# A row of 1 / rms for the gate: by way of HBM, in place of products with ones

## The chip, the cores and the metric

The kernel runs on one core of a Trainium2 chip. The metric is the device time of one execution in microseconds (us); each kernel is run several times and the median counts. The profile is of one execution by itself.

## The reference

One layer of a decoder on x of 1024 tokens by 1024 features, float32: an RMSNorm, gated linear attention (GLA) with 4 heads and chunks, a residual, another RMSNorm, a squared-ReLU MLP with 4096 hidden features, a residual, and a final RMSNorm. What the change touches is the gate of GLA:

```python
def rms_norm(x, g):
    y = x * lax.rsqrt(jnp.mean(x * x, axis=-1, keepdims=True) + EPS)
    return y * g
...
proj = h @ w_in                      # h = rms_norm(x, l0_norm_mix)
q, k, v, r, gk_low = jnp.split(proj, ...)
log_a = jax.nn.log_sigmoid(gk_low @ w_gk_up + b_gk) / GLA_GATE_NORM
```

gk_low has 16 columns (the gate's rank). 1 / rms is one number a token, and can be multiplied in after the product with w_in.

## The kernel before, in words

All big matrix products are done as seven products of half-sized blocks (Strassen's scheme), each of them in three passes of high and low parts so that float32 is kept. `step` does one such product: 4 lanes of 128 rows, each 4 times 3 matmuls of 128x512, so 48 matmuls. `chunks_of` runs a plan of such groups of seven steps; while step n runs on TensorE (PE), the operands of the next one are made by ScalarE (ACT, `split`: the high part) and VectorE (DVE: the low part; line 178: sums of blocks). `hooks` hang other work into a step: key (i, at) is the place before step `at` of group `i`, (i, at, "then") that after the next operands are made, and (i, at, lane, kp) a place between two matmuls of the step. The order on PE is the order in which the code is written; on the other engines a scheduler orders by the same program, and each queue, that of the DMA-issuing SyncE (SP) included, is worked off strictly in its order. DMAs share eight semaphores in turn, so a DMA also waits until the eighth one before it has landed.

Group 0 makes q and k, transposed (tokens in the free dimension), from the scaled but not normalized x; group 1 makes v. The split blocks of x are kept in HBM (`keep`, line 338, tiles xv: "keeps") and read back for group 1 (line 494). The loads of the weights for v are those of line 326.

What the gate needs, and the names that matter below:

- `gk_first` and `gk_second` multiply x's halves of 512 tokens with w_gk, transposed: the low-rank rows of the gate, with eight copies of 16 rows on 128 partitions, tokens along the free dimension.
- `token_rms` sums the squares of each token (ACT) and makes `rstd1` [128, 8], 1 / rms with the tokens on the partitions (`rstd_of`; its last instruction is line 114, DVE).
- The gate's rows have the tokens along the free dimension, so 1 / rms is needed as a row of 512 tokens on every partition. `spread_rms(hf)` makes it for one half: for each of 4 blocks of 128 tokens, DVE multiplies the identity with a column of `rstd1` (line 506), PE multiplies all ones with that (the product's rows are all the same: the diagonal), ACT copies the result from PSUM (line 508). Then DVE multiplies the gate's rows with it (line 513), ACT copies them to `gk` (line 514), and DVE leaves in partitions 64 to 127 the rest that the rounded copy lacks (line 515).
- `gate_in` multiplies `gk` with the split w_up (PE, "mm<-g,wup"), one matmul a head and half. The first one stands two lanes behind `spread_rms(0)`, within step 0 of group 1.

`spread_rms(0)` hangs at (1, 0, 0, 3), after the first lane of the first step for v; `spread_rms(1)` at (1, 5), after `gk_second`. In the order below and in the trace, "g" is a buffer of [128, 1024], "gl" and "mm" are PSUM banks, "big" holds a split operand, "wa" and "wb" weights, "vx" inputs and v.

Of the kernel before, what the change touches and what calls it, by code (L numbers as in the profile page):

```python
# [8 lines left out]
F32 = mybir.dt.float32  # L9
# [4 lines left out]
AF = mybir.ActivationFunctionType  # L14
ALU = mybir.AluOpType

P = 128
T = 1024
# [22 lines left out]
def order_after(tc, inst, other, wait=True):  # L41

    kind = mybir.DependencyClass.Sync if wait else mybir.DependencyClass.NoSync
    tc.add_manual_dep(inst.ins, other.ins.name, mybir.DependencyInfo(kind, mybir.DependencyReason.DATA),
                      reason="order of phases")
# [3 lines left out]
def hybrid_trunk(ctx: ExitStack, tc: tile.TileContext, x, xT, w_head, w_r, w_gk, w_up,  # L49
                 w_out, w_ff1, w_ff2, vecs, g_fin, out):  # L50
    nc = tc.nc
    act, dve, pe, pool = nc.scalar, nc.vector, nc.tensor, nc.gpsimd
    sb = ctx.enter_context(tc.tile_pool(name="sb", bufs=1))
    dram = ctx.enter_context(tc.tile_pool(name="dram", bufs=1, space=bass.MemoryType.DRAM))
# [5 lines left out]
    def new(tag, dtype=F32):  # L60
        count[0] += 1
        pool_ = ps if tag in ("mm", "gl") else sb
        return pool_.tile(SHAPE.get(tag, [P, 1024]), dtype, tag=tag, bufs=BUFS[tag], name=f"{tag}{count[0]}")

    def f32(ap):
        return ap.bitcast(F32)

    def mm(o, w, m, start, stop, partial=False):

        pe.matmul(o, w, m, start=start, stop=stop, skip_group_check=partial)  # L70
# [18 lines left out]
    ones = sb.tile([P, P], F32, name="ones")  # L89
# [6 lines left out]
    ident = sb.tile([P, P], F32, name="ident")  # L96
# [6 lines left out]
    def rstd_of(y, ss, n, cnt):  # L103

        m, t = new("st")[:, 0:n], new("st")[:, 0:n]
        act.activation(y, ss, AF.Ln, scale=1.0 / cnt, bias=eps)
        act.activation(y, y, AF.Exp, scale=-0.5)
        dve.tensor_scalar(m, ss, -0.5 / cnt, -0.5 * EPS, op0=ALU.mult, op1=ALU.add)
        if n == 1:
            dve.scalar_tensor_tensor(t, y, y, m, op0=ALU.mult, op1=ALU.mult)  # L110
        else:
            dve.tensor_tensor(t, y, y, op=ALU.mult)
            dve.tensor_tensor(t, t, m, op=ALU.mult)
        dve.scalar_tensor_tensor(y, t, 1.5, y, op0=ALU.add, op1=ALU.mult)
# [4 lines left out]
    def run(general):  # L119
        stat = {n: sb.tile([P, w], F32, tag=n, bufs=1, name=f"{n}{int(general)}")  # L120
                for n, w in dict(ss1=8, rstd1=8, ss2=8, rstd2=8, rstd3=8, tok=32, est=96).items()}
        ss1, rstd1, ss2, rstd2, rstd3 = (stat[n] for n in ("ss1", "rstd1", "ss2", "rstd2", "rstd3"))
# [5 lines left out]
        def half(hf):  # L128
            return slice(hf * 512, hf * 512 + 512)
# [291 lines left out]
        box = {}  # L421
# [9 lines left out]
        def token_rms(ts):  # L431
            for t in ts:
                xr = new("g4")
                nc.sync.dma_start(xr, x[t * P:(t + 1) * P, :])
                order_after(tc, act.activation(xr, xr, AF.Square, accum_out=ss1[:, t:t + 1]), last["split"], wait=False)
            if TT - 1 in ts:
                rstd_of(rstd1, ss1, 8, D)
                dve.tensor_tensor(r_sq, rstd1, rstd1, op=ALU.mult)
                dve.tensor_scalar(r_qs, r_sq, QS, None, op0=ALU.mult)
                dve.tensor_scalar(r_neg, rstd1, -1.0, None, op0=ALU.mult)  # L440
                dve.tensor_scalar(r_ss, r_sq, QS * QS / DV, None, op0=ALU.mult)

        qk, part = {}, {}

        def qk_view(a, h):

# [51 lines left out]

        def spread_rms(hf):

            u = new("g4")
            dg, rbc = u[:, 0:512], u[:, 512:1024]
            pb = new("mm")
            for c in range(4):
                cs = slice(c * P, c * P + P)
                dve.tensor_scalar(dg[:, cs], ident, rstd1[:, hf * 4 + c:hf * 4 + c + 1], None, op0=ALU.mult)
                mm(pb[:, cs], ones, dg[:, cs], True, True)
            act.activation(rbc, pb, AF.Copy)
            if hf == 0:
                box["gk"] = new("g4", F32R)  # L510
            raw, gk = box["raw"][hf], box["gk"][:, half(hf)]
            dst = raw if hf == 0 else dg
            dve.tensor_tensor(dst, raw, rbc, op=ALU.mult)
            act.activation(gk, dst, AF.Copy)
            dve.tensor_tensor(gk[64:128, :], dst[64:128, :], f32(gk[64:128, :]), op=ALU.subtract)
# [240 lines left out]
        def g(f, *args):  # L756
            return lambda: f(*args)
# [35 lines left out]
        def gk_second():  # L793
# [3 lines left out]
        wv = weight_side(True, from_v, dve, late=True)  # L797
        fine_steps.add((0, 0))
        hooks = {(0, 1): (gk_first,), (0, 3): (split_up,),
                 (0, 4): (g(token_rms, range(0, 4)),), (0, 5): (g(token_rms, range(4, 8)),),  # L800
                 (1, 0, 0, 3): (g(spread_rms, 0),),
                 (1, 2): (x12_load,), (1, 4): (x12_split,), (1, 5): (gk_second, g(spread_rms, 1))}
        if not general:
            hooks.update({(1, 0, 2, 3): (g(gate_in, 0, 0, "mm"), g(gate_in, 1, 0, "mm")),
                          (1, 0, 3, 3): (g(gate_in, 2, 0, "mm"),),
                          (1, 1, 0, 1): (g(gate_in, 3, 0, "mm"), g(prep_fast, 0, 0)),
                          (1, 2): (x12_load,),
                          (1, 2, "then"): (g(prep_fast, 1, 0),), (1, 3, "then"): (g(prep_fast, 2, 0),),
                          (1, 4): (), (1, 4, "then"): (g(prep_fast, 3, 0), x12_split),
                          (1, 5): (gk_second, g(spread_rms, 1)) + tuple(g(load_wr, 0, kq, "wa") for kq in range(4)),  # L810
                          (1, 6): tuple(g(f, a, kq, *tag) for f, a, kq, tag in
                                        [(split_wr, 0, kq, ()) for kq in range(4)]
                                        + [(load_wr, 1, kq, ("wa" if kq > 1 else "raw",)) for kq in range(4)]),
                          (1, 6, 2, 1): (g(gate_in, 0, 1, "mm"), g(prep_fast, 0, 1)),
                          (1, 6, 3, 1): (g(operands, 0, "mm"),)})
# [231 lines left out]
    with tc.manual_schedule(engines={mybir.EngineType.PE}):  # L1047
        run(False)
# [3 lines left out]
    with tc.If(go_general > 0):  # L1052

        level_mask = {}
        masks = new("at").bitcast(BF16)
        pool.memset(masks, 1.0)
        for n, s in enumerate(LEVELS):
            nb = 64 // s
            m = masks[:, n * 64:(n + 1) * 64].unsqueeze(1)
            mv = m.rearrange("p o (b t) -> p (o b) t", t=s)  # L1060
            pool.affine_select(mv, mv, [[-2 * s, nb], [0, s]], ALU.is_ge, 0.0, base=0, channel_multiplier=1)
            pool.affine_select(mv, mv, [[2 * s, nb], [0, s]], ALU.is_ge, 0.0, base=s - 1, channel_multiplier=-1)
            level_mask[s] = m
        run(True)
# [50 lines left out]
```

## Time and profile before

| | |
|---|---|
| median of 3 runs | 1020.11 us (1019.8 to 1021.35) |
| the profiled execution | 1020.24 us |
| its span, first to last instruction | 1018.4 us |
| PE busy | 1002.9 us, 98% |
| DVE, ACT, POOL busy | 721.9, 548.4, 191.2 us |
| mean granted TensorE clock | 0.995 |

A profile's line of a group or of the timeline gives the start (us from the start of the span), the length, the engine, the line of the kernel, the operation, and out<-in; in square brackets stands for how long the engine was idle before it, and who released it. PEld is the loading of weights, beside PE. SPq rows are DMAs being issued by SP: their length is the time of issuing, and the time until the data has landed is an answer of its own, on the DMAs. Float32 matmuls whose operands are not split are two records each.

### The profile page before, as it was taken

The page shows a single profiled execution, that of the slowest core. Times are in us where ns is not written, and L with a number is a line of the kernel's source. Part 1 is how long each engine was busy: PE and PEld are TensorE (multiplying, and loading weights), DVE is VectorE, ACT ScalarE, POOL GpSimd, SP SyncE. Part 2 cuts the span into 40 slices and gives each one's busy share as a digit, 9 for nine tenths or more (in the row PEclk, how much of TensorE's full clock was granted, in tenths as well). Part 3 has the DMA queues.
Part 4 walks back from the last instruction along what each step waited for, and adds up shares of the span by engine and source line. Part 5 has one row for each costly group of instructions (what it writes and reads, how often), then busy time and mean ns, then how long its engine had stood idle before and what let it go on. Part 6 is the DMA issues. An engine that isn't in the chain of part 4 may idle for free.

```text
span 1018.4 us, 12257 instructions
## 1 busy us (share of the span) xinstructions
PE 1002.9 (98%) x4618; PEld 835.9 (82%) x4618; DVE 721.9 (71%) x897; ACT 548.4 (54%) x828; POOL 191.2 (19%) x114
## 2 busy tenths in 40 slices
PE   8999999999999999999999999999999999999996
PEld 7788878888888888888888888888888888888884
DVE  4996686776568997979965338965339965339965
ACT  6785566666576457658332447332447332447355
POOL 0000010000000000041304341214341214341260
PEclk9999999999999999999999999999999999999998
DMA  8799796223236034573124762124762124861004
GB/s 266 277 332 378 268 305 192 83 84 104 83 92 200 20 104 181 210 283 133 42 83 165 283 236 101 42 83 165 285 244 91 41 83 165 294 240 45 1 1 169
DMA packets 103580, 164.28 MB, mean 161 GB/s; under 512 B 5336, under 2 KB 75096, under 8 KB 93272
## 3 DMA queue, kind: packets, MB, share of 16 engines
q1 hardware_dynamic: 102424, 162.75, 45.9%
q8 instruction: 38, 0.62, 0.2%
q10 hardware_dynamic: 1088, 0.67, 0.2%
q14 instruction: 30, 0.25, 0.1%
HBM read 127.74 MB, written 35.65 MB: 160 GB/s over the span
## 4 chain that ended last, share of the span: by engine, by line
PE 83%; DVE 1%; ACT 1%; issue 1%; ACTq 0%; DVEq 0%
PE gl L70 50%; PE mm L70 31%; PE mm L937 1%; PE gl L706 1%; PE gl L626 0%; DVE vx L902 0%; DVE big L82 0%; DVE g L927 0%; ACT g L1007 0%; ACT st L1008 0%; DVE st L1011 0%; ACT st L1009 0%; DVE g L1015 0%; PE mm L706 0%; ACT raw L1013 0%
## 5 line engine op out<-in xcount | busy, mean ns | idle before, releaser
L70 PE MATMUL gl<-big,big 128*128 128x512 f32 x2508 | 585.5, 390 | 3.3 <-ACT big L81 1.9
L70 PEld LDWEIGHTS gl<-big,big 128*128 128x128 f32 x2508 | 470.7, 188 | 101.6 <-DVE big L82 2.2
L70 PE MATMUL mm<-big,big 128*128 128x512 f32 x1188 | 279.7, 389 | 0.0
L70 PEld LDWEIGHTS mm<-big,big 128*128 128x128 f32 x1188 | 223.0, 188 | 46.3
L82 DVE TENSOR_TENSOR big<-wa,big 128x1024 fp32r<-128x1024 f32 (+1 forms) x118 | 159.4, 1377 | 107.1 <-ACT big L81 107.1
L81 ACT ACTIVATE big<-wa 128x1024 fp32r<-128x1024 f32 (+1 forms) x118 | 118.1, 1038 | 136.6 <-PE gl L70 66.6
L178 POOL TENSOR_TENSOR wa<-wa,wb 128x1024 f32<-128x1024 f32 x14 | 42.9, 3068 | 350.6 <-DVE big L82 350.6
L178 POOL TENSOR_TENSOR wa<-wa,wa 128x1024 f32<-128x1024 f32 x28 | 74.7, 2675 | 160.9 <-DVE big L82 159.6
L70 PE MATMUL mm<-big,wb 128*128 128x512 f32 x384 | 94.9, 397 | 0.0
L82 DVE TENSOR_TENSOR big<-hq,big 128x1024 fp32r<-128x1024 f32 x48 | 61.3, 1282 | 42.9 <-ACT big L81 42.8
L82 DVE TENSOR_TENSOR big<-wb,big 128x1024 fp32r<-128x1024 f32 x42 | 56.4, 1355 | 44.5 <-ACT big L81 44.3
L70 PEld LDWEIGHTS mm<-big,wb 128*128 128x128 f32 x384 | 70.6, 188 | 14.3
L81 ACT ACTIVATE big<-hq 128x1024 fp32r<-128x1024 f32 x48 | 48.5, 1052 | 54.0 <-PE gl L70 32.5
L81 ACT ACTIVATE big<-raw 128x1024 fp32r<-128x1024 f32 x44 | 45.7, 1058 | 55.3 <-DVE raw L178 28.3
L81 ACT ACTIVATE big<-wb 128x1024 fp32r<-128x1024 f32 x42 | 43.0, 1052 | 59.9 <-PE mm L70 33.2
L82 DVE TENSOR_TENSOR big<-raw,big 128x1024 fp32r<-128x1024 f32 x44 | 69.2, 1587 | 2.0 <-ACT big L81 2.0
L902 DVE TENSOR_TENSOR vx<-gl,vx 128x512 f32<-128x512 f32 x95 | 63.2, 681 | 6.1 <-PE gl L70 5.9
L178 POOL TENSOR_TENSOR wa<-wb,wa 128x1024 f32<-128x1024 f32 x14 | 41.1, 2947 | 44.7 <-DVE big L82 44.7
L546 POOL COPY top<-g 128x4 f32<-128x4 f32 x8 | 4.1, 518 | 204.4 <-DVE g L538 204.4
L960 ACT ACTIVATE hq<-hq 128x1024 f32<-128x1024 f32 x24 | 25.4, 1058 | 29.6 <-DVE hq L953 29.6
L70 PE MATMUL gl<-wb,wa 128*128 128x256 f32 x180 | 31.2, 304 | 0.0
L902 DVE TENSOR_TENSOR vx<-mm,vx 128x512 f32<-128x512 f32 x45 | 29.9, 680 | 1.5 <-PE mm L70 1.4
(183 smaller groups left out, 796.4 us busy)
## 6 DMA issues: line engine op xcount, KB each, us to landing
big<-xw SPq DMA_DIRECT2D x42, 1024.0 KB, 6.9
xv<-big SPq DMA_DIRECT2D x14, 1024.0 KB, 7.6
xw<-big SPq DMA_DIRECT2D x14, 1024.0 KB, 5.0
big<-xv SPq DMA_DIRECT2D x10, 1024.0 KB, 6.5
wb<-xv SPq DMA_DIRECT2D x32, 256.0 KB, 3.4
wb<-in_w_ff SPq DMA_DIRECT2D x32, 256.0 KB, 3.3
wa<-in_w_ff SPq DMA_DIRECT2D x32, 256.0 KB, 3.9
wa<-in_w_ff SPq DMA_DIRECT2D x16, 512.0 KB, 4.8
```

Source lines behind the costliest of these rows:

```text
L70: pe.matmul(o, w, m, start=start, stop=stop, skip_group_check=partial)
L81: last["split"] = act.activation(hi, src, AF.Copy)
L82: last["low"] = dve.tensor_tensor(lo, src, f32(hi), op=ALU.subtract)
L178: op = self.eng.tensor_tensor(*(self.ap(b, kp, 2) for b in (o, x_, y_)), op=op)
L546: pool.tensor_copy(top[:, 8 * h + 4 * hf:8 * h + 4 * hf + 4].unsqueeze(2), a[:, :, P - 1:P])
L706: pe.transpose(tp[:, h * P:(h + 1) * P], on[:, h * DV + j * P:h * DV + j * P + P], ident)
L902: return dve.tensor_tensor(xd, p_, xd, op=ALU.add)
L937: pe.transpose(p_[:, c * P:(c + 1) * P], xn[4 * hf + c][:, kt * P:(kt + 1) * P], ident)
L960: act.activation(d2, d2, AF.Relu)
```

## The change

The four products with ones and their diagonals are gone. `token_rms` stores `rstd1` to a row of 1024 numbers in HBM as soon as it is final (`rms_row`, a DMA on SP's queue, 128 partitions of 8 numbers, each number a piece of 4 bytes by itself, since neighbours on a partition are 128 tokens apart). `load_rms(hf)` reads 512 of them back onto all 128 partitions (256 KB into a g buffer, SP's queue). It hangs at (0, 6, "then") for the first half, and behind `x12_split` in (1, 4, "then") for the second. `spread_rms` multiplies with what was read. The hooks that run on this data are those under `if not general`.

```diff
@@ token_rms @@
                 rstd_of(rstd1, ss1, 8, D)
+                nc.sync.dma_start(rms_row.rearrange("o (t p) -> p (o t)", p=P), rstd1)
                 dve.tensor_tensor(r_sq, rstd1, rstd1, op=ALU.mult)
...
-        qk, part = {}, {}
+        rms_row = dram.tile([1, T], F32, name=f"rms{int(general)}")
+
+        def load_rms(hf):
+
+            if hf == 0:
+                box["rbc"] = {}
+            box["rbc"][hf] = new("g4")[:, 0:512]
+            nc.sync.dma_start(box["rbc"][hf], rms_row[:, half(hf)].to_broadcast([P, 512]))
+
+        qk = {}
...
         def spread_rms(hf):
 
-            u = new("g4")
-            dg, rbc = u[:, 0:512], u[:, 512:1024]
-            pb = new("mm")
-            for c in range(4):
-                cs = slice(c * P, c * P + P)
-                dve.tensor_scalar(dg[:, cs], ident, rstd1[:, hf * 4 + c:hf * 4 + c + 1], None, op0=ALU.mult)
-                mm(pb[:, cs], ones, dg[:, cs], True, True)
-            act.activation(rbc, pb, AF.Copy)
+            raw, rbc = box["raw"][hf], box["rbc"][hf]
             if hf == 0:
                 box["gk"] = new("g4", F32R)
-            raw, gk = box["raw"][hf], box["gk"][:, half(hf)]
-            dst = raw if hf == 0 else dg
+            gk = box["gk"][:, half(hf)]
+            dst = raw if hf == 0 else rbc
             dve.tensor_tensor(dst, raw, rbc, op=ALU.mult)
             act.activation(gk, dst, AF.Copy)
...
-                 (0, 4): (g(token_rms, range(0, 4)),), (0, 5): (g(token_rms, range(4, 8)),),
+                 (0, 4): (g(token_rms, range(0, 4)),), (0, 5): (g(token_rms, range(4, 8)),), (0, 6, "then"): (g(load_rms, 0),),
...
-                          (1, 4): (), (1, 4, "then"): (g(prep_fast, 3, 0), x12_split),
+                          (1, 4): (), (1, 4, "then"): (g(prep_fast, 3, 0), x12_split, g(load_rms, 1)),
```

The order on SP's queue, from the loads of v's weights (wa, wb, from in_w_head) to the end of the keeps (xv), in the kernel before:

```order
L326 DMA wb79_644<-in_w_head 128x2x256 x2
L326 DMA wb80_645<-in_w_head 128x2x256 x2
L338 DMA xv600_102<-big83_658 128x2048
L338 DMA xv610_103<-big84_661 128x2048
L326 DMA wa85_718<-in_w_head 128x2x256 x2
L326 DMA wa86_719<-in_w_head 128x2x256 x2
L326 DMA wb87_724<-in_w_head 128x2x256 x2
L326 DMA wb88_725<-in_w_head 128x2x256 x2
L338 DMA xv000_90<-big89_730 128x2048
L338 DMA xv010_91<-big90_731 128x2048
L338 DMA xv500_100<-big93_796 128x2048
L338 DMA xv510_101<-big94_797 128x2048
```

and the same place in the changed kernel, from the last of the first eight loads on (line 438 is the store of `rstd1`, line 451 the load of the row):

```order
L326 DMA wb80_647<-in_w_head 128x2x256
L438 DMA rms0_194<-rstd10_84 128x8x1
L326 DMA wb80_647<-in_w_head 128x2x256
L338 DMA xv600_102<-big83_660 128x2048
L338 DMA xv610_103<-big84_663 128x2048
L326 DMA wa85_720<-in_w_head 128x2x256 x2
L326 DMA wa86_721<-in_w_head 128x2x256 x2
L326 DMA wb87_726<-in_w_head 128x2x256 x2
L326 DMA wb88_727<-in_w_head 128x2x256 x2
L338 DMA xv000_90<-big89_732 128x2048
L338 DMA xv010_91<-big90_733 128x2048
L451 DMA g493_746<-rms0_194 128x512
```

The store has gone between the two halves of the eighth tile's loads (the seventh and the eighth load of 256 KB), and the load of the row between the second keep and the third of the last four. The store waits for `rstd1` to be final (line 114 on DVE), the load for the store's landing.

The order on ACT, where step 0 of group 1 is emptied from PSUM (line 476 before, 486 after: one bank a lane, into v's tile) and the gate's rows are copied to gk (line 514 before, 517 after); lines 527 and 528, or 530 and 531, read the first products with w_up. Before:

```order
L476 ACTIVATE vx100_827<-gl99_814,tok0_88 128x512
L508 ACTIVATE g4101_829<-mm102_830 128x512
L476 ACTIVATE vx105_857<-gl104_844,tok0_88 128x512
L514 ACTIVATE g4103_840<-g436_293 128x512
L476 ACTIVATE vx107_872<-gl106_859,tok0_88 128x512
L527 ACTIVATE g4109_876<-mm108_874,vec_63 128x512
```

and in the changed kernel:

```order
L486 ACTIVATE vx101_831<-gl100_818,tok0_88 128x512
L486 ACTIVATE vx104_850<-gl103_837,tok0_88 128x512
L486 ACTIVATE vx106_865<-gl105_852,tok0_88 128x512
L517 ACTIVATE g4102_833<-g436_294 128x512
L530 ACTIVATE g4108_869<-mm107_867,vec_63 128x512
L531 ACTIVATE g4108_869<-mm107_867,vec_63 128x512
```

The copy to gk has moved behind the emptying of the third lane. On DVE the sequence around it is as before, without the four products with the identity: the two sums of line 178, the multiplication of the gate's rows (line 513 before, 516 after), the subtraction (515, now 518).

More of the change, by code (lines that the diff above doesn't have):

```diff
@@ L799, in run @@
         hooks = {(0, 1): (gk_first,), (0, 3): (split_up,),
-                 (0, 4): (g(token_rms, range(0, 4)),), (0, 5): (g(token_rms, range(4, 8)),),
+                 (0, 4): (g(token_rms, range(0, 4)),), (0, 5): (g(token_rms, range(4, 8)),), (0, 6, "then"): (g(load_rms, 0),),
                  (1, 0, 0, 3): (g(spread_rms, 0),),
-                 (1, 2): (x12_load,), (1, 4): (x12_split,), (1, 5): (gk_second, g(spread_rms, 1))}
+                 (1, 2): (x12_load,), (1, 4): (x12_split, g(load_rms, 1)), (1, 5): (gk_second, g(spread_rms, 1))}
         if not general:
```

## Prediction

> **What bounds the kernel now.** The page comes first, then what PE waited for in the whole span.
>
> ```profile
> span 1018.4 us, 12257 instructions
> PE 1002.9 (98%) x4618; PEld 835.9 (82%) x4618; DVE 721.9 (71%) x897; ACT 548.4 (54%) x828; POOL 191.2 (19%) x114
> ```
> ```profile
> PE gl L70 <- ACT big L81: 1.9, 1, 1.9
> ...
> PE mm L70 <- DVE vx L474: 0.9, 1, 0.9
> ```
>
> TensorE is busy for 98% of the span, and its few waits are single ones of 1 to 2 us (columns: total, times, longest). So a microsecond taken from PE's queue is a microsecond won, and a new wait in that queue is lost in full: nothing later stands idle to give it back. The change touches PE's queue twice, so those two places are read in the timelines. PE first (start, length; one matmul with ones is two records, hence x8 for four):
>
> ```profile
> 93.45 1.05 PE L70 MATMUL mm<-g,ones 128*128 128x128 f32 x8
> 94.26 5.72 PE L70 MATMUL gl<-big,big 128*128 128x512 f32 x24
> 99.82 0.62 PE L70 MATMUL mm<-g,wup 128*128 128x512 f32 x2
> ...
> 152.10 1.05 PE L70 MATMUL mm<-g,ones 128*128 128x128 f32 x8
> 152.91 17.28 PE L70 MATMUL gl<-big,big 128*128 128x512 f32 x75
> ```
>
> PE goes straight through: the products with ones take from 93.45 to 94.26 and from 152.10 to 152.91, and 5.6 us after the first group come the gate's products with w_up (99.82), which read what spread_rms made. What DVE and ACT do for those:
>
> ```profile
> 79.30 0.16 DVE L114 SCALAR_TENSOR_TENSOR rstd<-st,rstd 128x8 f32<-128x8 f32 x1
> ...
> 94.79 2.36 DVE L178 TENSOR_TENSOR wa<-wa,wb 128x1024 f32<-128x1024 f32 x2
> 97.06 0.68 DVE L513 TENSOR_TENSOR g<-g,g 128x512 f32<-128x512 f32 x1
> 98.54 0.69 DVE L515 TENSOR_TENSOR g<-g,g 64x512 fp32r<-64x512 f32 x1 [0.80 <-ACT g L514]
> ```
> ```profile
> 97.30 0.69 ACT L476 ACTIVATE vx<-gl,tok 128x512 f32<-128x512 f32 x1 [2.16 <-PE gl L70]
> 97.89 0.62 ACT L514 ACTIVATE g<-g 128x512 fp32r<-128x512 f32 x1
> 100.02 0.69 ACT L476 ACTIVATE vx<-gl,tok 128x512 f32<-128x512 f32 x1 [1.51 <-PE gl L70]
> ```
>
> The gate's rows are ready when L515 ends, 98.54 + 0.69 = 99.23, and PE wants them at 99.82: 0.6 us of slack, no more. rstd1, the start of it all, is final at 79.46. That date matters for SP, whose queue the change uses:
>
> ```profile
> 76.06 0.87 SPq L338 DMA_DIRECT2D xv<-big  x2
> ...
> 87.61 2.58 SPq L338 DMA_DIRECT2D xv<-big  x4
> ```
>
> **Removed.** Two groups of products with ones: 94.26 - 93.45 = 0.81 us each, 1.62 us off PE. The eight DVE products with the identity and two ACT copies out of PSUM go too; I cost them at nothing, since DVE then waits for other work (the first group stands ahead of splits that wait for ACT's).
>
> **Added on SP: the store.** It is issued behind seven of the eight loads of wv (the order in the change, above), and waits there for L114, until 79.5. In the kernel before, SP came to this point between the seventh load (74.75 + 0.55, below) and the two keeps at 76.06. So SP stands for some 4 us, and behind it wait the eighth load, the keeps, eight more loads, four keeps and the row's own load. What does that do to the DMA rings? The seventh load and its landing (us from issue, last column of the second answer):
>
> ```profile
> 74.75 0.55 SPq L326 DMA_DIRECT2D wb<-in_w_head  x1
> ```
> ```profile
> wb<-in_w_head SPq DMA_DIRECT2D x1, 256.0 KB, 5.0
> ```
>
> It lands at 79.8, so the rings run dry just as the store goes out. After a keep a load of 256 KB lands 0.7 us later when the rings are full (keep issued 76.56, landed after 10.3; load issued 77.39, landed after 10.2), but 3.4 us after its issue when they are empty:
>
> ```profile
> 76.56 0.37 SPq L338 DMA_DIRECT2D xv<-big  x1
> 77.39 0.39 SPq L326 DMA_DIRECT2D wa<-in_w_head  x1
> 130.23 0.51 SPq L717 DMA_DIRECT2D wa<-in_w_r  x1
> ```
> ```profile
> xv<-big SPq DMA_DIRECT2D x1, 1024.0 KB, 10.3
> wa<-in_w_head SPq DMA_DIRECT2D x1, 256.0 KB, 10.2
> wa<-in_w_r SPq DMA_DIRECT2D x1, 256.0 KB, 3.4
> ```
>
> Before, the eighth load landed at about 79.8 + 0.7 = 80.5. After: store issued at 79.5, 0.8 us of issuing (the 512 pieces of the row at 130.23 took 0.51; the store has 1024), load issued at 80.3, landed 3.4 later at 83.7. The 1024 pieces of 4 bytes of the store stand ahead of it. No row here shows such a store. From below: nothing, because they move while the rings are idle anyway, and the smallest load, 128 rows of 88 bytes, lands like any other:
>
> ```profile
> vec<-in_vecs ACTq DMA_DIRECT2D x1, 11.0 KB, 3.5
> ```
>
> From above: a keep writes 128 rows of 8 KB to HBM in 2.4 us when the rings are full (below), 19 ns a row, and 1024 such rows would be 19 us. In between, 2 KB at a keep's rate are 4.8 ns, so 1024 are 4.9 us. The pieces are nearest to the smallest rows: w_r's 512 pieces pass within the 0.7 us of 256 KB, 1024 thus in 1.4 at most, and I take the middle of 0 and 1.4. Then the eighth load lands at 83.7 + 0.7 = 84.4, and everything behind it is 84.4 - 80.5 = **3.9 us late**. Who misses that? The eighth load feeds DVE's splits just ahead of L178 (94.79): nobody. The eight loads behind the keeps feed L178; they had landed by 92.8 (a keep queued behind them landed at 95.2, below, less its own 2.4), so now by 96.7, against 96.0 for L178's second half: 0.7 us on DVE, inside the wait that follows. The Trainium skill, page "DMA: Bandwidth & Descriptors", speaks against this store: by its Rules for kernel authors a strided last dim becomes one descriptor per element, and by its Specifications less than 512 B is a read-modify-write. No run here shows that yet; with the roughly 10.5 ns a packet of its section Bandwidth, 64 on each of 16 engines would be an estimate of 0.7 us.
>
> **Added on SP: the load of the row.** It stands behind the first two of the four keeps that began at 87.61. The first two of them landed so:
>
> ```profile
> 88.36 0.34 SPq L338 DMA_DIRECT2D xv<-big  x1
> ```
> ```profile
> xv<-big SPq DMA_DIRECT2D x1, 1024.0 KB, 7.6
> xv<-big SPq DMA_DIRECT2D x1, 1024.0 KB, 9.2
> ```
>
> that is at 87.61 + 7.6 = 95.2 and 88.36 + 9.2 = 97.6. The row's 256 KB follow 0.7 later, at 98.3 without the lateness: already past 97.06, when DVE wants them. With it the row lands at 98.3 + 3.9 = 102.2.
>
> **Moved on ACT.** In the new order ACT empties the third bank of the step before it copies the gate's rows. PE finishes that bank just before the w_up products, now at 99.82 - 0.81 = 99.0. The emptying starts 0.2 later (100.02 against 99.82), the copy 0.6 after that (97.89 - 97.30), DVE's subtraction 0.65 after that (98.54 - 97.89) and lasts 0.69: 101.1. So PE waits at least 101.1 - 99.0 = **2.1 us** even for a row that is on time.
>
> **The wait.** With the row at 102.2: multiplication (0.68), copy (0.65 to the subtraction), subtraction (0.69), and the handing over: 104.3. PE is there at 99.0, and waits 5.3 us. Behind the multiplication in DVE's queue stands the emptying of the next step's banks, which PE has yet to fill, so DVE's standing still costs nothing more.
>
> **The clock.** PE's gap is long enough for the clock (columns: length, PE busy, PEld, DVE, ACT, POOL, granted clock, DMA, GB/s):
>
> ```profile
> 4.75:8.16 3.41, 1.46 (x8) 0.85 (x8) 1.80 (x4) 1.35 (x2) 0.42 (x2) 1.00 0.99 311
> 8.16:11.57 3.41, 3.41 (x9) 2.64 (x10) 2.65 (x5) 2.52 (x5) 0.00 (x0) 0.50 0.88 259
> ```
>
> With 1.46 of 3.41 us busy, that is after a gap of 1.95 us, the next 3.41 us were granted half the clock: 9 matmuls where 15 would fit (24 take 5.56 us at 94.26). A gap of 5.3 us leaves such a stretch nearly empty, so I add half of 3.41, less what of it falls into the gap itself: between 0 and 1.7, taken as 1.2. The Trainium skill, "TensorE: Matmul & The Clock Gate", Part 1, gives the same consequence for an idle window of about 3.4 us; in this trace 1.95 us sufficed, and the measurement decides.
>
> **The second half** (152 us). Its row is loaded behind the last x12 store, which lands at 155.5:
>
> ```profile
> 149.90 0.53 SPq L791 DMA_DIRECT2D xv<-g  x1
> ```
> ```profile
> xv<-g SPq DMA_DIRECT2D x1, 512.0 KB, 5.6
> ```
> ```profile
> 153.82 0.69 DVE L513 TENSOR_TENSOR g<-mm,g 128x512 f32<-128x512 f32 x1
> 154.77 1.23 DVE L82 TENSOR_TENSOR big<-wb,big 128x1024 fp32r<-128x1024 f32 x1 [0.25 <-ACT big L81]
> ```
>
> The row lands near 156.2, DVE waits 2.4 us, and the split behind it (154.77) ends near 158.2. PE needs that split only in the next step, 48 of the 75 matmuls at 152.91 later, near 164. Hidden by 5 us; the 0.81 us stay won.
>
> **The sum**, against the profiled execution's own 1020.24 us: - 1.62 + 5.3 + 1.2 = + 4.9, **1025.1 us**. The median of the runs is 0.13 lower, which is left out.
>
> **Rivals.**
> One, not slower: the row comes in time. If the rings lose nothing at 79.5 because the next data follow at once, the row lands at 98.3, and ACT's 2.1 us is all: 1020.24 - 1.62 + 2.1 = 1020.7 (1021.9 if that gap costs the clock too). It decides where the row lands before about 99.9, a lateness under 1.6 us. For it: the store goes out 0.3 us before the rings run dry. The Trainium skill has it as a rule ("DMA: Bandwidth & Descriptors", Rules for kernel authors: a DMA issued early and waited for late hides its fixed cost behind compute). Against it: the 3.4 us of a load on empty rings. 12%.
> Two, the store is slow: pieces at a full row's 19 ns put 19 us in place of 0.7, and the wait grows to some 23: 1043. 8%.
> Three, the second row is late by more than 5 us, behind w_r's loads, and DVE's split holds PE at 164: 1 to 3 us on top, 1027. 4%.
> My own case keeps 76%. Its low end is a store that costs no issuing and no rows (79.5 + 3.4 = 82.9, 2.4 late, a wait of 3.8), no loss of clock, and half of PE's 0.9 us wait at 148 (L474, the second list above) saved by the shifted work: - 1.6 + 3.8 - 0.4, 1022.0. Its high end is the store at 4.9 us and a second slow stretch of the clock: + 4.2 + 1.2, 1030.5. That range leaves out rivals one and two.
>
> A measurement of this kernel tells about 0.2%, 2.0 us, from no change. Slower by more than that are my case and rivals two and three, less the lowest part: 0.86. Within it is rival one and that part: 0.12. Faster would need the row in time and PE's 0.9 us wait at 148 gone as well, and even that is 1019.8: 0.02.
>
> **What would show it.** In the profile after: PE idle before the first mm<-g,wup, released by DVE's subtraction (line 518), 5.3 us, with a slice at half clock behind it; SP issuing nothing from 75.3 to 79.5; DVE idle before line 516, released by the DMA g<-rms, which lands near 102; the second line 516 waiting 2 us with PE undisturbed. The prediction is wrong if PE's gap is near 2 us with ACT ahead of the copy (rival one), if the store's landing takes over 8 us (two), or if PE stalls near 164 (three).

## The result, and the profile after

The changed kernel takes **1031.49 us** (median of 5 runs, 1030.86 to 1032.82), the kernel before 1020.11 us (5 runs). The ratio is 1.0111, 95% interval 1.0098 to 1.0125: slower by some 11 us, where 4.9 were forecast, and 1 us above the forecast range. The profiled execution is the median one, 1031.49 us. Its span, and what PE waited for between 80 and 115 us (total, times, longest):

```profile
span 1029.7 us, 12221 instructions
PE 1004.6 (98%) x4602; PEld 836.3 (81%) x4602; DVE 721.1 (70%) x889; ACT 548.1 (53%) x826; POOL 191.2 (19%) x114
```
```profile
PE mm L70 <- DVE g L518: 7.1, 1, 7.1
PE gl L70 <- ACT hq L469: 3.2, 1, 3.2
```

Both waits are new. The first was forecast (5.3 us); of the second the prediction knew nothing. PE's timeline has them in the step in which the gate's products stand (idle time before the instruction in brackets):

```profile
87.66 6.05 PE L70 MATMUL gl<-big,big 128*128 128x512 f32 x26
96.93 7.37 PE L70 MATMUL gl<-big,big 128*128 128x512 f32 x24 [3.21 <-ACT hq L469]
111.40 1.22 PE L70 MATMUL mm<-g,wup 128*128 128x512 f32 x2 [7.11 <-DVE g L518]
```

Follow both back to their start. SP's queue, and what SP waited for:

```profile
73.70 1.82 SPq L326 DMA_DIRECT2D wb<-in_w_head  x3
79.59 0.37 SPq L438 DMA_DIRECT2D rms<-rstd  x1
80.00 0.58 SPq L326 DMA_DIRECT2D wb<-in_w_head  x1
80.69 1.27 SPq L338 DMA_DIRECT2D xv<-big  x2
```
```profile
SPq L438 <- DVE rstd L114: 4.0, 1, 4.0
SPq L326 <- DMA rms<-rstd: 2.9, 1, 2.9
```

The store is issued at 79.59 in 0.37 us, after 4.0 us of standing, and the eighth load (the second of tile wb80, which is the fourth tile of weights, not the eighth) follows at 80.00: 0.3 us earlier than forecast. Its landing is what differs (the DMA answers; last column: us from issue to landing; first the eighth load, then the first keep behind it):

```profile
wb<-in_w_head SPq DMA_DIRECT2D x1, 256.0 KB, 12.5
```
```profile
xv<-big SPq DMA_DIRECT2D x1, 1024.0 KB, 14.6
```

The load lands at 92.5 instead of the forecast 84.4, the keep at 95.3. In between the DMA rings (the 16 DMA engines with what is queued at them) hardly move anything, as the stretches of the span show (the last two columns: busy share of the DMA engines, GB/s):

```profile
80.00:81.50 1.50, 1.50 (x8) 1.27 (x7) 1.50 (x5) 1.35 (x2) 0.00 (x0) 1.00 0.32 3
81.50:90.00 8.50, 8.50 (x39) 7.02 (x39) 3.59 (x5) 1.73 (x2) 0.00 (x0) 1.00 0.26 19
90.00:92.00 2.00, 2.00 (x11) 1.65 (x10) 0.00 (x0) 0.00 (x0) 0.00 (x0) 1.00 0.59 160
92.00:95.00 3.00, 1.72 (x8) 1.10 (x6) 0.00 (x0) 0.00 (x0) 0.00 (x0) 1.00 1.04 438
```

The same 8.5 us in the kernel before:

```profile
81.50:90.00 8.50, 8.50 (x39) 7.06 (x38) 5.40 (x10) 4.08 (x6) 0.00 (x0) 1.00 1.04 369
```

So for most of 10 us behind the store's issue the rings carry 19 GB/s in place of 369, with the eighth load and two keeps, 2.25 MB, queued by 82. Below, the rings are called closed while that lasts. They don't wait for the store's packets to be sent: in 0.7 us from 80.5 on, the DMA answer counts 1033 packets under 512 bytes, about as many as the store has pieces.

```profile
DMA packets 1033, 0.00 MB, mean 6 GB/s; under 512 B 1033, under 2 KB 1033, under 8 KB 1033
```

Who misses that? First ACT. Its timeline before, the landing of the first keep before (issued at 76.06), and ACT's timeline after:

```profile
85.49 2.01 ACT L81 ACTIVATE big<-vx 128x1024 fp32r<-128x1024 f32 x2 [3.43 <-PE gl L70]
```
```profile
xv<-big SPq DMA_DIRECT2D x1, 1024.0 KB, 7.6
```
```profile
85.59 1.06 ACT L81 ACTIVATE big<-vx 128x1024 fp32r<-128x1024 f32 x1 [3.43 <-PE gl L70]
95.34 1.06 ACT L81 ACTIVATE big<-vx 128x1024 fp32r<-128x1024 f32 x1 [8.68 <-DMA xv<-big]
96.30 2.04 ACT L469 ACTIVATE hq<-gl 128x512 f32<-128x512 f32 x4
...
110.00 0.63 ACT L517 ACTIVATE g<-g 128x512 fp32r<-128x512 f32 x1 [4.98 <-DVE g L516]
```

The second of the two splits writes a "big" buffer that the keep xv600 still has to read. Before, that keep landed at 83.7, 2.8 us ahead of the second split (half of 2.01 behind 85.49: 86.5); now it lands at 95.3, and ACT stands 8.68 us. Behind it in ACT's queue are the four emptyings of PSUM banks (line 469), and at 93.7 PE has no free bank: the 3.21 us. Then the row itself, its load's landing, and DVE's sums and two steps:

```profile
g<-rms SPq DMA_DIRECT2D x1, 256.0 KB, 9.2
```
```profile
102.36 2.60 DVE L178 TENSOR_TENSOR wa<-wa,wb 128x1024 f32<-128x1024 f32 x2 [0.69 <-DMA wb<-in_w_head]
109.28 0.69 DVE L516 TENSOR_TENSOR g<-g,g 128x512 f32<-128x512 f32 x1 [4.32 <-DMA g<-rms]
110.66 0.69 DVE L518 TENSOR_TENSOR g<-g,g 64x512 fp32r<-64x512 f32 x1 [0.69 <-ACT g L517]
```

The row's load is issued at 100.08 and lands at 109.3, against 102.2 forecast. The row is not the whole of PE's 7.1 us: DVE's sums, late themselves behind ACT's split and late weights, end at 104.96, so with a row on time DVE would have multiplied 4.3 us earlier, and PE would still have waited some 2.8 us (an estimate from these rows; PE is there at 104.29, and starts 2.1 us behind the start of the multiplication). Each of PE's gaps is followed or overlapped by half clock (columns: length, PE, PEld, DVE, ACT, POOL, granted clock, DMA, GB/s):

```profile
97.20:100.62 3.42, 3.42 (x9) 2.68 (x9) 1.75 (x3) 3.42 (x6) 0.00 (x0) 0.50 1.09 364
...
107.44:114.27 6.83, 2.87 (x7) 2.29 (x8) 1.38 (x2) 2.67 (x5) 0.00 (x0) 0.50 0.96 396
```

PE was busy for 3.42 and 2.87 us of these, and half of that is lost: 3.1 us. The sum: - 1.62 (ones) + 3.2 + 7.1 + 3.1 - 0.9 (PE's wait at 148 for L474 is gone) = + 10.9 us; the spans differ by 1029.7 - 1018.4 = 11.3. The second half is as forecast in kind: its row is late for DVE, by 4.7 us where 2.4 were forecast, and PE has no wait from 125 to 185 us.

```profile
170.21 0.69 DVE L516 TENSOR_TENSOR g<-mm,g 128x512 f32<-128x512 f32 x1 [4.67 <-DMA g<-rms]
```

### The profile page after: what moved, and what is told of

It reads as the page before. It is cut to its first block, busy times and chain, and to the rows that moved or that the text cites. A ratio compares the mean times of both kernels' runs of the same rounds, so it can differ in the third digit from the quotient of the medians.

```text
span 1029.7 us, 12221 instructions
## 1 busy us (share of the span) xinstructions
PE 1004.6 (98%) x4602; PEld 836.3 (81%) x4602; DVE 721.1 (70%) x889; ACT 548.1 (53%) x826; POOL 191.2 (19%) x114
## 4 chain that ended last, share of the span: by engine, by line
PE 89%; DMA 4%; DVE 2%; SPq 2%; issue 1%; ACT 1%; DVEq 0%; ACTq 0%
PE gl L70 53%; PE mm L70 34%; DMA wa<-in_w_head 3%; DMA wb<-in_w_head 1%; DMA g<-rms 1%; SPq L326 1%; PE mm L940 1%; DVE big L82 1%; PE gl L709 1%; SPq L314 0%; PE gl L629 0%; DVE vx L905 0%; SPq L312 0%; DVE wa L178 0%; DVE g L930 0%
```

## The experiments

The theory after the result, A: the store's pieces of 4 bytes close the rings, each at a price, and all else follows. It was to be told from a cost of the load, of SP's standing, and of the order on ACT. Times are medians; the ratio is to the kernel before on the same chip, with its 95% interval.

**The store in wide pieces.** 128 pieces of 32 bytes; the tokens of the row then stand in another order.

```diff
-nc.sync.dma_start(rms_row.rearrange("o (t p) -> p (o t)", p=P), rstd1)
+nc.sync.dma_start(rms_row.rearrange("o (p t) -> p (o t)", p=P), rstd1)
```

> The changed kernel with the store in 128 pieces of 32 bytes (a partition's 8 numbers next to each other in HBM) in place of 1024 pieces of 4; the row that comes back then holds the tokens' numbers in another order, so only its time is of use. Theory A (the rings are closed by the number of pieces, about 10 us for 1024, so about 1.2 us for 128): the load behind the store lands about 4.5 us after its issue in place of 12.5, the row near 103 in place of 109.3, ACT's split no longer waits for a keep and PE's 3.2 us wait for ACT goes, PE's wait for the gate's rows is about 5.5 us: 1025 to 1026 us. Rival B (what counts is SP's standing for rstd1 and the refilling of the rings, whatever the pieces): as the changed kernel, 1031.

1023.35 us, ratio 1.0031 (1.0020 to 1.0043): 8 us less than the change, and 2 less than A expected. The eighth load, and the only wait of PE between 80 and 120 us:

```profile
wb<-in_w_head SPq DMA_DIRECT2D x1, 256.0 KB, 5.3
```
```profile
PE mm L70 <- DVE g L518: 4.4, 1, 4.4
```

The eighth load lands at 85.2 (forecast 84.4), the row at 101.4 (102.2), PE waits 4.4 us (5.3), and no wait for ACT is left. With a store that costs little, the prediction's whole chain is there, and rival B, by which the time would be that of the change, falls. The 2 us are that shorter wait (4.4 in place of A's 5.5) and PE's 0.9 us wait at 148, which is gone here too.

**Half the pieces.** Columns 0 to 3 only, 512 pieces; both loads read that half.

```diff
+nc.sync.dma_start(rms_row[:, 0:512].rearrange("o (t p) -> p (o t)", p=P), rstd1[:, 0:4])
```

> The changed kernel, but only 4 of the 8 columns are stored, 512 pieces of 4 bytes, and both loads read that half (so the second half of the gate's rows is scaled with the wrong tokens' numbers). Theory A: the store closes the rings for half as long, 5 us in place of 10; the row lands near 104.5, PE's wait for ACT's emptying goes, that for the gate's rows is about 7.5 us: 1027 to 1028 us. Rival B: 1031.

1030.34 us, ratio 1.0098 (1.0081 to 1.0115); the eighth load lands 12.0 us after its issue. Half the pieces cost all but the same: A's price for each piece falls.

**The store alone**, the products with ones kept.

> The kernel before, with the store of rstd1 added at the same place of SP's queue and nothing else: the row is never read, the products with ones stay. Theory A: the load behind the store lands 12 us after its issue, ACT's split waits 8 to 9 us for a keep, PE 3 us for ACT, and DVE's sums at line 178 wait for late weights, so that the gate's rows come 2 to 3 us late as well; with the clock 1026 to 1028 us. Rival (the recorded forecast of a store that costs 0.7 us on the rings and makes all 3.9 us late): only 0.7 us at line 178, 1020 to 1021.

1027.45 us, ratio 1.0067 (1.0050 to 1.0084). The eighth load takes 12.7 us, ACT waits for the keep as in the change, and PE waits twice, without any row being read:

```profile
95.96 1.06 ACT L81 ACTIVATE big<-vx 128x1024 fp32r<-128x1024 f32 x1 [8.84 <-DMA xv<-big]
```
```profile
PE mm L70 <- DVE g L517: 4.2, 1, 4.2
PE gl L70 <- ACT hq L461: 2.5, 1, 2.5
```
```profile
97.05 1.23 DVE L82 TENSOR_TENSOR big<-vx,big 128x1024 fp32r<-128x1024 f32 x1 [8.67 <-ACT big L81]
99.94 2.36 DVE L82 TENSOR_TENSOR big<-wb,big 128x1024 fp32r<-128x1024 f32 x2 [1.67 <-DMA wa<-in_w_head]
102.89 2.59 DVE L178 TENSOR_TENSOR wa<-wa,wb 128x1024 f32<-128x1024 f32 x2 [0.59 <-DMA wb<-in_w_head]
```

Most of the loss is thus the store's, by way of other tensors' transfers. PE's 4.2 us come from DVE: by its timeline, the sums of line 178, ahead of the gate's multiplication, are late, first by ACT's late split and then by late weights. How much each of the two counts is not separated by this run.

**The load alone.** No store; the row is read from x's first token, so the gate's numbers are others. SP never stands.

```diff
-nc.sync.dma_start(box["rbc"][hf], rms_row[:, half(hf)].to_broadcast([P, 512]))
+nc.sync.dma_start(box["rbc"][hf], x[0:1, half(hf)].to_broadcast([P, 512]))
```

> The changed kernel without the store: the row is read from the first token of x, at the same places of SP's queue, so the gate's rows are scaled with other numbers. Theory A with the order on ACT as worked out (the copy of the gate's rows stands behind the emptying of the third lane): the row lands near 98.3, PE waits 2.1 us for DVE's subtraction and gains 1.6: 1020.7 us, up to 1022 if the clock answers. Rival: the order on ACT costs nothing and the products' 1.6 us are won: 1018.5. Rival: the row alone, behind two keeps, is already the whole cost: above 1025.

1020.26 us, ratio 1.0004 (0.9992 to 1.0017): no difference. PE's wait is the forecast's floor of 2.1 us, from the order on ACT:

```profile
PE mm L70 <- DVE g L517: 2.0, 1, 2.0
```

It cost no half clock. In these traces the clock changes after stretches of 3.41 us or a multiple (4.75 to 8.16 and 8.16 to 11.57 before; 3.42 and 6.83 us in the change), and this gap lies in two of them:

```profile
98.25:101.66 3.41, 2.61 (x12) 1.83 (x10) 1.39 (x2) 1.38 (x3) 0.00 (x0) 1.00 1.01 411
101.66:105.07 3.41, 2.19 (x9) 1.80 (x10) 0.69 (x1) 2.09 (x4) 0.00 (x0) 1.00 0.83 336
```

PE was busy for 2.61 and 2.19 us of these; in the stretch at the start of the kernel before, which was followed by half clock, for 1.46.

**What makes the pieces dear.** Theory C takes the place of A's price for each piece: pieces that lie close together in HBM are served one after another. The loads in the following kernels read x, as above. First, 1024 pieces of 4 bytes, each in 512 bytes of its own:

```diff
-rms_row = dram.tile([1, T], F32, name=f"rms{int(general)}")
+rms_row = dram.tile([T, 128], F32, name=f"rms{int(general)}")
+nc.sync.dma_start(rms_row.rearrange("(t p) c -> p t c", p=P)[:, :, 0:1], rstd1.unsqueeze(2))
```

> The store keeps its 1024 pieces of 4 bytes, but each goes to a 512-byte row of its own in a larger HBM buffer; the two loads read the first token of x in place of the row, so the gate's products get other numbers and SP isn't held for the store's landing. Theory C (4-byte pieces are slow only where many of them fall close together in HBM, since they are then served one after another): the eighth load lands 4 to 7 us after its issue, as with the wide store (5.3), and the time is 1022 to 1024.5 us. Rival A (each 4-byte piece is slow by itself, wherever it goes): the eighth load lands 11 to 13 us after its issue, PE waits about 3 us for the hq evictions, and the time is 1028 to 1031 us.

1023.63 us, ratio 1.0032 (1.0020 to 1.0043), the eighth load 4.0 us after its issue, near the 3.4 us that the prediction had for empty rings:

```profile
wb<-in_w_head SPq DMA_DIRECT2D x1, 256.0 KB, 4.0
```

So neither the width of 4 bytes nor the number of 1024 is dear in itself. Then 128 pieces side by side, one column of rstd1:

```diff
+nc.sync.dma_start(rms_row[:, 0:P].rearrange("o (t p) -> p (o t)", p=P), rstd1[:, 0:1])
```

> Only the first column of 1 / rms is stored: 128 pieces of 4 bytes into one stretch of 512 bytes; the two loads read the first token of x in place of the row, so the gate's products get other numbers. Theory C: 128 pieces that share one stretch close the rings about as long as eight such stretches side by side do; the eighth load lands 10 to 12.5 us after its issue and the time is 1027 to 1030.5 us. Rival A (a price for each piece): an eighth of the pieces costs an eighth of the 9 us, the eighth load lands 5 to 6.5 us after its issue, and the time is 1021.5 to 1024 us. A fixed price of any store that is written in 4-byte pieces would give the same as theory C here, and 1028 to 1031 in the kernel with rows of their own.

1030.42 us, ratio 1.0101 (1.0081 to 1.0121). An eighth of the pieces closes the rings nearly as long as all of them:

```profile
wb<-in_w_head SPq DMA_DIRECT2D x1, 256.0 KB, 11.1
```

**Another queue.** The change with its store on GpSimd's queue, so that SP doesn't stand:

```diff
+nc.gpsimd.dma_start(rms_row.rearrange("o (t p) -> p (o t)", p=P), rstd1)
```

> The changed kernel, with the store on GpSimd's queue, so that SP isn't held 4.0 us for L114 and its loads are issued as before the change; the row is stored and read as in the change. If the pieces close the rings for every queue (all queues share the 16 DMA engines): the transfers that stand in the rings at 80 us land 8 to 10 us late, the keep xv600 near 92 instead of 83.6, PE waits 2 to 5 us for the hq evictions and 4 to 7 us for the gate's row, and the time is 1025 to 1031 us. If only the store's own queue is held: the loads land as before the change, the row is on time but for the 2.1 us of ACT's order, and the time is 1020 to 1022 us.

1028.22 us, ratio 1.0090 (1.0067 to 1.0113). The eighth load and the first keep (landed 81.8) were through before the store came, so PE doesn't wait for ACT, other than expected, and its wait for the gate's rows is longer than the 4 to 7 us expected. But the second keep, on SP's queue, which took 10.3 us before, is held by a store on another queue:

```profile
xv<-big SPq DMA_DIRECT2D x1, 1024.0 KB, 18.4
```
```profile
PE mm L70 <- DVE g L518: 9.2, 1, 9.2
```

So the store closes the rings for SP's queue too. The Trainium skill has it that queues are not separate in this ("DMA: Bandwidth & Descriptors", Issuing engines are not separate DMA queues: whichever engine starts a DMA, it runs on the same 16 DMA engines); this run agrees, with 18.4 us in place of 10.3.

**How close, how many.** Two theories were left: pieces are served in turn within 512 bytes (C512), or within 64 (C64). First 64 pieces in each of eight stretches of 512 bytes (partitions 0 to 63), and 16 pieces in 64 bytes:

```diff
+nc.sync.dma_start(rms_row.rearrange("o (t p) -> p (o t)", p=P)[0:64, :], rstd1[0:64, :])
...
+nc.sync.dma_start(rms_row[:, 0:16].rearrange("o (t p) -> p (o t)", p=16), rstd1[0:16, 0:1])
```

> Only partitions 0 to 63 of 1 / rms are stored: 512 pieces of 4 bytes, 64 into the first half of each of the eight 512-byte stretches; the loads read the first token of x in place of the row, so the gate's products get other numbers. The runs so far leave open how wide the stretch is in which pieces are served one after another. Theory C512 (512 bytes: 128 pieces in turn, about 9 us / 128 = 0.07 us each): 64 in turn close the rings for 4.5 us, the eighth load lands 7.5 to 9.5 us after its issue, and the time is 1024.5 to 1027 us. Theory C64 (64 bytes: 16 pieces in turn, about 9 us / 16 = 0.56 us each): each full 64-byte stretch still takes 16, the eighth load lands 11 to 12.5 us after its issue, and the time is 1027 to 1031 us.

1030.84 us, ratio 1.0112 (1.0097 to 1.0127), eighth load after 11.8 us: C512 falls.

> Only 16 pieces of 4 bytes are stored, into 64 bytes; the loads read the first token of x in place of the row, so the gate's products get other numbers. Theory C512: 16 pieces in turn are about 1.1 us, the eighth load lands 4.5 to 6 us after its issue, and the time is 1022 to 1024 us, as with the wide store. Theory C64: 16 pieces in turn are the whole 9 us, the eighth load lands 10 to 12.5 us after its issue, and the time is 1027 to 1031 us.

1024.59 us, ratio 1.0054 (1.0038 to 1.0069); by its time a little above, by its eighth load within what C512 had for it, and far from C64, which falls here:

```profile
wb<-in_w_head SPq DMA_DIRECT2D x1, 256.0 KB, 5.9
```

As neither explains both, three more: 1024 pieces 64 bytes apart (the buffer is [T, 16]), 64 pieces side by side, and 128 pieces of 16 bytes side by side.

> 1024 pieces of 4 bytes as in the change, but 64 bytes apart in a larger HBM buffer; the loads read the first token of x in place of the row, so the gate's products get other numbers. Side by side the pieces make the eighth load land 11 to 12.5 us after its issue, 512 bytes apart 4.0. Theory D64 (they collide where they share 64 bytes): here none do, the eighth load lands 4 to 6 us after its issue and the time is 1022 to 1024.5 us. Theory D512 (they collide where they share 512 bytes; here eight do): the eighth load lands 8 to 12.5 us after its issue and the time is 1025 to 1031 us.

1023.68 us, ratio 1.0037 (1.0023 to 1.0051), as D64 had it. A distance of 64 bytes is enough to take the price away, with all 1024 pieces:

```profile
wb<-in_w_head SPq DMA_DIRECT2D x1, 256.0 KB, 4.1
```

> 64 pieces of 4 bytes side by side in 256 bytes; the loads read the first token of x in place of the row, so the gate's products get other numbers. 16 pieces made the eighth load land 5.9 us after its issue, 128 pieces 11.1, 1024 pieces 12.5. If the price grows with the pieces up to about 128 (by the line through 16 and 128): 8 us after its issue, and 1025 to 1027 us. If it is one jump that comes once there are enough of them: 10.5 to 11.5 us and 1027.5 to 1030.5 us, or else 5 to 6.5 us and 1022 to 1025 us where 64 are still too few.

1027.94 us, ratio 1.0082 (1.0066 to 1.0099). The load is 1 us above the line through 16 and 128 pieces, and apart from both jumps, so by the load the price grows with the pieces; the time, above the 1025 to 1027 us of that theory, lies in the range of the higher jump and doesn't tell them apart.

```profile
wb<-in_w_head SPq DMA_DIRECT2D x1, 256.0 KB, 9.0
```

> 128 pieces of 16 bytes side by side in 2 KB; the loads read the first token of x in place of the row, so the gate's products get other numbers. 128 pieces of 4 bytes side by side made the eighth load land 11.1 us after its issue, 128 pieces of 32 bytes 5.3. If each piece that isn't a full 32 or 64 bytes is dear where it has neighbours: 10 to 12 us and 1027 to 1030.5 us. If the price goes by how many pieces share the same 64 bytes (4 here, 16 with 4 bytes): a quarter of the 6 us, 5.5 to 7 us after its issue, and 1022 to 1025 us.

1024.44 us, ratio 1.0043 (1.0026 to 1.0060), the eighth load after 6.0 us: four pieces to 64 bytes are cheap, as expected of a price that goes by how many share them. It can't go by that alone, since 16 pieces of 4 bytes in one stretch of 64 bytes cost no more. All of them together:

| pieces of the store | eighth load lands after its issue, us | PE's waits from 80 to 120 us, us | ratio |
|---|---|---|---|
| 1024 of 4 bytes, 512 bytes apart | 4.0 | 4.3 | 1.0032 |
| 1024 of 4 bytes, 64 bytes apart | 4.1 | 4.2 | 1.0037 |
| 128 of 32 bytes, side by side | 5.3 | 4.4 | 1.0031 |
| 128 of 16 bytes, side by side | 6.0 | 5.2 | 1.0043 |
| 16 of 4 bytes, side by side | 5.9 | 5.1 | 1.0054 |
| 64 of 4 bytes, side by side | 9.0 | 8.1 | 1.0082 |
| 128 of 4 bytes, side by side | 11.1 | 10.1 | 1.0101 |
| 512 of 4 bytes (64 by 8) | 11.8 | 10.5 | 1.0112 |
| 512 of 4 bytes (128 by 4) | 12.0 | 11.1 | 1.0098 |
| 1024 of 4 bytes, the change | 12.5 | 10.3 | 1.0111 |

The kernels differ in their loads: in the change, in the one of 32 bytes and in that of 128 by 4 the row's load waits for the store, in the others it doesn't. Landings and waits are from the profiled executions, the ratios from all runs; the profiled execution took 1028.14 us in the kernel with 512 bytes (median 1023.63) and 1027.52 in the one with 128 pieces of 4 bytes (median 1030.42).

**A version with wide pieces in the right order.** PE transposes rstd1 to 8 rows of 128 tokens, DVE copies them, GpSimd's queue stores 8 pieces of 512 bytes and reads the row; `spread_rms(0)` hangs at (1, 0, "then").

```diff
+tp = new("mm")
+pe.transpose(tp[0:8, 0:P], rstd1, ident)
+with tc.high_priority():
+    dve.tensor_copy(row8, tp[0:8, 0:P])
+    pool.dma_start(rms_row.rearrange("o (t p) -> (o t) p", p=P), row8)
-nc.sync.dma_start(box["rbc"][hf], rms_row[:, half(hf)].to_broadcast([P, 512]))
+pool.dma_start(box["rbc"][hf], rms_row[:, half(hf)].to_broadcast([P, 512]))
...
-(1, 0, 0, 3): (g(spread_rms, 0),),
+(1, 0, "then"): (g(spread_rms, 0),),
```

> A version meant to beat both: PE transposes 1 / rms to 8 rows of 128 tokens, DVE copies them, and GpSimd's queue stores 8 pieces of 512 bytes and reads the row back; the first of the two spread steps stands one place earlier, so that ACT's copy to gk lies between the hq evictions instead of behind the w_up block. Theory (small pieces and the ACT order are the whole cost): no load is late by more than 1.5 us, PE doesn't wait before the gate's products by more than 0.5 us, and 1.6 us of products less one transposition of about 0.1 us are gained: 1018 to 1019.5 us. Rival (an extra 256 KB in the rings at this place costs by itself, by making the keeps or w_up's weights late): 1020 to 1023 us, with a PE wait behind L81 or the hq evictions.

**1016.89 us** beside 1019.66, ratio 0.9975 (0.9965 to 0.9986): faster than both, and by 1 us more than expected, since PE's 0.9 us wait at 148 us is gone here too. DVE stands 7.2 us for the row, but it lands at 95.6, ahead of PE, which comes to the gate's products at 98.4; ACT's copy stands ahead of the last emptyings, and PE goes through without a wait:

```profile
95.60 0.69 DVE L522 TENSOR_TENSOR g<-g,g 128x512 f32<-128x512 f32 x1 [7.18 <-DMA g<-rms]
```
```profile
96.32 0.63 ACT L523 ACTIVATE g<-g 128x512 fp32r<-128x512 f32 x1 [8.04 <-DVE g L522]
96.86 1.07 ACT L475 ACTIVATE hq<-gl 128x512 f32<-128x512 f32 x2
```
```profile
79.17 0.27 PE L452 MATMUL mm<-ident,rstd 128*8 128x128 f32 x1
79.20 19.33 PE L70 MATMUL gl<-big,big 128*128 128x512 f32 x84
98.37 0.61 PE L70 MATMUL mm<-g,wup 128*128 128x512 f32 x2
```

This version changes the pieces, the queue and the place of `spread_rms(0)` together; what each of them is worth in it was not taken apart.

**The same with `spread_rms(0)` back at (1, 0, 0, 3).**

> The version with 8 pieces of 512 bytes on GpSimd's queue, with the spread step back at the place that the change has, so that ACT's copy to gk stands behind the evictions of the w_up block again. The version with the early place took 1016.9 us beside 1019.7. If the 2.1 us of ACT's order are a cost of their own: PE waits about 2 us before the gate's products at about 98 us and the time is about 2 us above the early place, 1018.5 to 1020 us, no more than 1 us from the kernel before. If the early place matters little, since the row comes late anyway: within 0.5 us of 1017 us.

1017.38 us beside 1019.53, ratio 0.9977 (0.9967 to 0.9986). The wait of 2 us that was expected isn't there, but not because it costs nothing: the scheduler put ACT's copy ahead of the last emptyings (97.55, emptyings from 98.09) in this kernel as well. The place in the code didn't set the order, so this run tells nothing of the 2.1 us; the load alone does.

## Why the prediction was wrong, point by point

- **Failed: the price of the store on the rings.** The prediction took 0.7 us for the 1024 pieces of 4 bytes, by the rule that they are nearest to the smallest rows that the trace showed. In the change the eighth load lands 12.5 us after its issue; with as many such pieces, but 64 bytes apart, 4.1. In the prediction's terms (3.4 us on empty rings, and the store on top) the store costs 12.5 - 3.4 = 9.1 us, 13 times what was taken, above the 4.9 of the range's high end and below rival two's 19; 8.4 of it is what pieces side by side cost more than pieces 64 bytes apart. By the prediction's own sign (the store's landing over 8 us: SP's wait for it ended near 89.8, 10 us after the issue) rival two was the right kind, at less than half its price. All rows used as neighbours were reads, or wide writes; a narrow write to HBM was in none.
- **Failed: who else waits for late rings.** "Who misses that?" was asked of the weights' readers only. A keep reads an SBUF buffer, and ACT's split needs that buffer free: 2.8 us of slack before, 8.7 us short after. It costs PE 3.2 us and a stretch of half clock. The forecast's own 3.9 us of lateness were already past the slack, by 1.1 us; in the run with wide pieces the keep lands at 87.6, ACT stands 1.1 us for it, and PE has no wait there, so that much is covered.
- **Held: SP's standing**, 4.0 us for L114, with the rings dry behind it; **the row behind two keeps**: its own load takes 9.2 us as those keeps did, and with a cheap store lands at 101.4 (102.2 forecast).
- **Held: ACT's order as a floor of 2.1 us** even for a row on time: 2.0 in the load alone, which gave rival one's time, 1020.26 against 1020.7.
- **Mis-sized by what came before it: PE's wait.** 5.3 forecast, 4.4 with wide pieces, 7.1 in the change. The row there is 7.1 us later than forecast, but PE is 5.3 us late itself (104.3 in place of 99.0), nearly all of it by its other wait and the half clock behind that (3.2 + 1.7). The forecast had late weights cost DVE 0.7 us, hidden in the wait for the row; the late sums would have held PE for some 2.8 us by themselves.
- **Held in kind: the clock.** Each of the two gaps in the change brought half clock; with two gaps it is 3.1 us instead of 1.2.
- **Held: the 1.62 us of products** and **the second half's cover**. PE's 0.9 us wait at 148 is gone in every kernel tried, the one with the store alone included; the prediction had allowed half of it in its low end. It isn't tied to the products, then; what in the new order takes it away wasn't tried.

## What to carry to other kernels

Before a small tensor is sent through HBM, look at the shape of its pieces there: transposing it on chip, so that each partition writes one contiguous run, cost PE under 0.3 us here, and together with the DMAs on GpSimd's queue and ACT's copy ahead of the emptyings it turned 11 us of loss into a gain of 3. A DMA that stalls the rings is paid by whatever stands behind it on any queue, so list not only who reads the late loads but also who needs the buffers that late stores still hold. And where a price has no row of its own kind in the trace (a narrow write among reads), keep the far bound in the range instead of choosing the nearest row of another kind.

## What the runs showed of the hardware

- A store of 128 pieces of 4 bytes that stand side by side in HBM held up the load behind it by some 7 us (landing 11.1 us after its issue, against 4.1), one of 64 by 5, one of 16 by 2; from 128 to 1024 pieces 1.4 us are added (12.5). 1024 pieces 64 bytes apart cost no more than those 512 bytes apart (4.1 and 4.0). Narrow pieces between 4 and 64 bytes apart were not tried, so 64 bytes is an upper bound of the distance that is enough. By which part of the path to HBM neighbours hold each other up, and why eight times 128 cost little more than 128, no run here tells.
- The Trainium skill ("DMA: Bandwidth & Descriptors", Specifications) has read-modify-write below 512 bytes. That alone doesn't give these times: 4-byte pieces 64 bytes apart are below it too, and the load behind them lands after 4.1 us; side by side it is 12.5. The measurement decides.
- The clock: a gap of 2.02 us, spread over two stretches of 3.41 us (the load alone), brought no half clock, where 1.95 us inside one stretch did (the kernel before). So a gap's length alone does not tell what it costs. The two differ in how the gap lies against the stretches, which fits; whether anything else played a part was not tried.
